# A two-layer mixer step: wider first sums, and the last 512 output columns with tokens on partitions

## The chip, the cores and the metric

The kernel runs on one core of one Trainium2 chip. The metric is the time of one execution in microseconds (us), the median of a few runs. A profile is one further execution, recorded by the hardware profiler. TensorE's clock has two levels in it, 1.2 GHz (a granted clock of 0.50) and 2.4 GHz (1.00).

## What is computed

The reference takes 128 context tokens and 256 noisy latent tokens through two layers each and returns both outputs and the new keys and values. One layer, cut to what matters here:

```python
shift, scale, gate = split(silu(cvec) @ w_mod[l] + b_mod[l], 3)     # 2048 x 6144
h = rmsnorm(x, norm_g[l]) * (1 + scale) + shift                     # x: tokens x 2048
chunks = split(h @ w_in[l], 11)                                     # 2048 x 5632
...                                                                 # Fourier, pooling, attention, convolution
y = concatenate([y_f, y_p, y_a, y_c]) @ w_out[l]                    # 2048 x 2048
x = x + gate * y
...
y_out = rmsnorm(x, final_g)                                         # after the second layer
```

`rmsnorm` divides every token by the root of the mean of its 2048 squares, so no output element can be finished before all 2048 columns of `x` are known for its token.

## The kernel before

All 384 tokens are worked on together, channels on the 128 partitions and tokens along the free dimension: `xT[g][:, b, :]` holds channels `(4 g + b) * 128` and on, for 384 tokens. Tokens 0 to 127 are the context, 128 to 383 the latent ones; `SEG` keeps their modulation apart. Weights come as tiles of 512 KB (`wtile`, L227): a DMA into one of 5 `raw` buffers, then `halves` (L211) makes a rounded high part on ScalarE (L116) and the remainder on VectorE (L107), each 128x512, in 6 buffers `hi` and 6 `lo`. A product is three matmuls: high by high, high by low, low by high (`mm3`, L439). Loads of weights and their splits are issued with a higher priority than their place in the program (`ahead`, L208).

**The start.** The constants and the four input groups `xT` are loaded, 3 matmuls of zeros (`idle<-still,ones`, L167) run while they come, and squares of the input are added in pairs on VectorE (`xsq`). `token_sums` (L421) then sums squares over partitions: the squares are the stationary operand, the moving one is a single column of ones, for each of 3 blocks of 128 tokens. There are eight such calls, two for each input group; a full float32 matmul leaves two records in the trace, so they are 48 records (`ssq`, L423). Of the first four modulation items (`mod_item`, L255; 16 matmuls, 32 records, and one 512 KB load each) two stand between the sums of groups 2 and 3, and two behind the last sums, beside the square root, the reciprocal and the diagonal on the other engines. A matmul with that diagonal (`bc`, L418) spreads the result over partitions, `make_h` (L427) builds the first `h`, and the first matmul `mm` follows. The queues of TensorE and of the DMA engine SP keep the written order up to the end of the first four chunks; VectorE and ScalarE keep it up to the first `h`. Behind that, a scheduler orders each engine by priority at compile time.

**The end.** In the second layer the output projection runs over 4 groups of 512 columns. Groups 0 to 2 go over 8 weight tiles each with 4 accumulators (one for 128 columns). Group 3 goes over its 4 blocks of 128 columns one by one, so that one block's work behind the matmuls runs beside the next block's matmuls. `finish_block` (L914) adds gate times result to `xT`, squares it, adds the squares up in `sacc`, multiplies by `final_g`, and transposes the block on TensorE to tokens on partitions (`otp`, L931). After the last block, the sums over partitions (`st`, L423) give the root for each token, twelve tiles of 128x512 are multiplied by its reciprocal (L980, L982), and twelve stores of 256 KB follow on SP's queue (L987).

Of the kernel before, what the change touches and what calls it, by code (L numbers as in the profile page):

```python
# [8 lines left out]
F32 = mybir.dt.float32  # L9
F32R = mybir.dt.float32r  # L10
AF = mybir.ActivationFunctionType
# [3 lines left out]
P = 128  # L15
# [40 lines left out]
def mixer_step(  # L56
    ctx: ExitStack,
    tc: tile.TileContext,
    x_in, cache_k, cache_v, consts, lam, packs,
    y_prompt, y_sample, new_k, new_v,  # L60
):
    nc = tc.nc
# [30 lines left out]
    def nm(s):  # L93
        uid[0] += 1
        return f"{s}_{uid[0]}"
# [16 lines left out]
    def act(out, a, func, **kw):  # L112
        nc.scalar.activation(out=out, in_=a, func=func, **kw)  # L113
# [19 lines left out]
    ones = one.tile([P, P], F32, tag="ones", name="ones")  # L133
    nc.vector.memset(ones, 1.0)
    still = gtile("H", "still", (P, 512))
    nc.vector.memset(still, 0.0)
    eps_t = one.tile([P, 1], F32, tag="eps", name="eps_t")
    nc.vector.memset(eps_t, EPS)
    cmod = one.tile([P, KC, 32], F32, tag="cmod", name="cmod")
# [16 lines left out]
    act(cmod[:, :, 0], cview("c_ctx"), AF.Silu)  # L156
    act(cmod[:, :, 1], cview("c"), AF.Silu)
    warm = one.tile([P, 1], F32, tag="warm", name="warm")
    act(warm, cmod[:, 0, 2:3], AF.Sqrt, bias=eps_t[:, 0:1])
    ncol = cview("norm_g")  # L160
    bcol = cview("b_mod")

# [7 lines left out]
    for g in range(4):  # L170
        sq = gtile("M", "xsq0")
        xsq.append(sq)
        act(sq[:, 0:2, :], xT[g][:, 0:2, :], AF.Square)
        tt(sq[:, 2:4, :], xT[g][:, 2:4, :], xT[g][:, 2:4, :], ALU.mult)
        tt(sq[:, 0:2, :], sq[:, 0:2, :], sq[:, 2:4, :], ALU.add)

# [78 lines left out]
    def mod_item(l, segs, k0, nk):  # L255
        nb = sum(n for _, _, n in segs)
        w = nb * P
        if prio[0]:
            raw = rawp.tile([P, nk, nb, P], F32, tag="raw", name=nm("mraw"))
        else:  # L260
            raw = gtile("Y", "mraw", (P, nk, nb, P))
        with ahead():
            def rows(a):
                parts = []
                for kind, b0, n in segs:
                    c0 = MOD.index(kind) * D + b0 * P
                    parts.append(a[l, k0 * P:(k0 + nk) * P, c0:c0 + n * P].reshape(nk, P, n, P))
                import numpy as np
                return np.concatenate(parts, axis=2).transpose(1, 0, 2, 3)

            nc.sync.dma_start(out=raw, in_=packs["w_mod"].take(rows, (P, nk, nb, P)))
        key = (l, segs)
        if k0 == 0:
            mod_ps[key] = mdp.tile([P, 512], F32, tag="md", name=nm("mod"))
        ps = mod_ps[key]
        for j in range(nk):
            for q in range(4):
                qs = slice(32 * q, 32 * q + 32)
                nc.tensor.matmul(ps[qs, 0:nb * 32].rearrange("p (b n) -> p b n", n=32), lhsT=cmod[:, k0 + j, :],  # L279
                                 rhs=raw[:, j, :, qs], start=(k0 + j == 0), stop=(k0 + j == KC - 1))  # L280
        if k0 + nk == KC:
            del mod_ps[key]
            T = one.tile([P, 8, 32], F32, tag="S", name=nm("T"))
            nc.vector.transpose(out=T[:, 0:nb, :].rearrange("p b n -> p (b n)"), in_=ps[:, 0:nb * 32])
            o = 0
            for kind, b0, n in segs:
                mod_store(l, kind, b0, n, T[:, o:o + n, 0:2])
                o += n
# [127 lines left out]
    def bcast_tokens(dg):  # L416
        bc = sm("bc")
        nc.tensor.matmul(bc[:, :NT], lhsT=ones, rhs=dg.rearrange("p t k -> p (t k)"))  # L418
        return bc

    def token_sums(st, acc, start=True, stop=True):  # L421
        for t in range(TB):
            nc.tensor.matmul(st[:, t:t + 1], lhsT=acc[:, t * P:(t + 1) * P], rhs=ones[:, 0:1], start=start and t == 0,  # L423
                             stop=stop and t == TB - 1)
        return st[:, 0:TB]

    def make_h(l, xT, bc, kcs, hh, hl):  # L427
        for kc in kcs:
# [355 lines left out]
    for l in range(DEPTH):  # L784
        if l == 0:
            groups = [(0, 1), (1, 1)] + [(k, 2) for k in range(2, KC, 2)]
            first = mod_group(0, *groups[0])
            ssq = sm("ssq")
            for g in range(4):
                if g == 3:  # L790
                    for it in first[:2]:
                        mod_item(*it)
                for i in range(2):
                    stat = token_sums(ssq, xsq[g][:, i, :], g == 0 and i == 0, g == 3 and i == 1)
            dg = diagonal(rstd_cols(stat, TB, 1.0 / D))
            for it in first[2:]:
                mod_item(*it)
        else:
            dg = diagonal(rstd_cols(stat, TB, 1.0 / D))
        bc_ps = bcast_tokens(dg)  # L800
        bc = one.tile([P, NT], F32, tag="bs", name=nm("bcs"))
        if l:
            copy_a(bc, bc_ps[:, :NT])
# [110 lines left out]
        def finish_block(g, b, ps, outs):  # L914
            kc = 4 * g + b
            x = xT[g][:, b, :]
            for a, z, vv in SEG:
                stt(x[:, a:z], ps[:, a:z], GT[l][:, kc, vv:vv + 1], x[:, a:z], ALU.mult, ALU.add)
            if kc == 0:
                act(sacc, x, AF.Square)  # L920
            else:
                sq = tmpp.tile([P, NT], F32, tag="t1", name=nm("xsq"))
                act(sq, x, AF.Square)
                if kc < KC - 1:
                    tt(sacc, sacc, sq, ALU.add)
                else:
                    tots.append(token_sums(tots[0], sq, start=False))
            if final:
                copy_a(x, x, scale=col("final_g", kc))
                for t in range(TB):  # L930
                    nc.tensor.transpose(outs[t][:, b * P:(b + 1) * P], x[:, t * P:(t + 1) * P], ident)  # L931

        otk = []
        for g in range(4):
            ps4 = [mmp.tile([P, 512], F32, tag="mm", name=nm("mm")) for _ in range(4)]
            if g < 3:
                for i, kt in enumerate(order):
                    hi, lo = wtile(w_src("w_out", l, 2 * kt, g * BR))
                    main_tile(ps4, hi, lo, (2 * kt, 2 * kt + 1), yh, yl, i == 0, i == 7)
                    pump()  # L940
            outs = [sm("otp") for _ in range(TB)] if final else None
            for b in range(4):
                if g == 3:
                    c0 = g * BR + b * P
                    for k0 in range(0, KC, 8):
                        hi, lo = wtile(w_src("w_out", l, k0, c0, 8, P), shape=(P, 8, P))
                        for j in range(8):
                            kc = k0 + j
                            mm3(ps4[b][:, :NT], hi(j), lo(j), yh[kc // 4][:, kc % 4, :],
                                yl[kc // 4][:, kc % 4, :], kc == 0, kc == KC - 1)  # L950
                        pump()
                        if b == 3 and k0 == 0:
                            tots.append(mdp.tile([P, 512], F32, tag="md", name=nm("st")) if final else sm("st"))
                            token_sums(tots[0], sacc, stop=False)
                finish_block(g, b, ps4[b], outs)
            if not final:
                nc.sync.dma_start(out=xd[g], in_=xT[g])
            elif g < 3:
                ot = gtile("H", "ot", (P, TB, BR))
                for t in range(TB):  # L960
                    nc.scalar.copy(out=ot[:, t, :], in_=outs[t])
                otk.append([ot[:, t, :] for t in range(TB)])
            else:
                otk.append(outs)
        pump(flush=True)
        rate["pe"] = rate["dve"] = 0.0
        if not final:
            share(1, [("gate", b0) for b0 in range(0, KC, 4)], NG)
            pe_mods(NB1)
        stat = tots[1]  # L970
        if not final:
            pe_mods(NB2)

    r = rstd_cols(stat, TB, 1.0 / D)
    n = 0
    for g in range(4):
        res = gtile("H", "res", (P, TB, BR))
        for t in range(TB):
            if n % 5 in (1, 3):
                copy_a(res[:, t, :], otk[g][t], scale=r[:, t:t + 1])  # L980
            else:
                nc.vector.tensor_scalar(out=res[:, t, :], in0=otk[g][t], scalar1=r[:, t:t + 1], scalar2=None,  # L982
                                        op0=ALU.mult)
            n += 1
            cs = slice(g * BR, (g + 1) * BR)
            dst = y_prompt[0, :, cs] if t == 0 else y_sample[0, (t - 1) * P:t * P, cs]
            nc.sync.dma_start(out=dst, in_=res[:, t, :])  # L987


def shape_constants():  # L990
# [115 lines left out]
```

## Time and profile before

| what | value |
|---|---|
| time, median of 3 runs | 1249.11 us (1248.88 to 1251.1) |
| time of the profiled execution | 1249.6 us |
| its span, first to last instruction | 1247.8 us |
| mean granted TensorE clock | 0.986 |
| TensorE busy in matmuls | 1223.0 us |
| VectorE, ScalarE busy | 922.4 us, 550.3 us |
| last matmul of the projection begins | 1233.37 us |

The profiled execution's own time is 1.8 us above its span. Moments below are counted from the span's start. A record's duration contains the filling of the array; what a matmul costs in a row of matmuls is read from the starts of consecutive ones.

### The profile page before, as it was taken

How to read it: one execution, taken by the hardware profiler on the slowest of the kernel's cores; microseconds unless marked ns; L12 is line 12 of the kernel's file. 1: busy time of each engine (PE TensorE's matmuls, PEld its weight loads, DVE VectorE, ACT ScalarE, POOL GpSimd, SP SyncE). 2: the span in 40 equal slices, each digit the busy share in tenths (PEclk: the TensorE clock that was granted, in tenths of full speed). 3: DMA queues.
4: the chain of work that ended last, by engine and by line, in shares of the span. 5: the costliest groups of instructions: out<-in, count | busy, mean ns of one | idle time of the engine just before them, and what ended most of it. 6: DMA issues, size and time to landing. Idle time of an engine off the chain costs nothing.

```text
span 1247.8 us, 22061 instructions
## 1 busy us (share of the span) xinstructions
PE 1223.0 (98%) x8558; PEld 1148.6 (92%) x8558; DVE 922.4 (74%) x1774; ACT 550.3 (44%) x1103; POOL 2.1 (0%) x34
## 2 busy tenths in 40 slices
PE   8999999999999999999999999999999999999995
PEld 6899998898999999999998999989999999999995
DVE  4787879999957956989968469997464895647452
ACT  3433333444547644433335433334455755344442
POOL 0000000000000000000000000000000000000000
PEclk6999999999999999999999999999999999999998
DMA  8988886553346766988945444444232563645322
GB/s 302 351 314 318 304 306 236 171 175 122 132 169 218 281 228 221 330 302 319 326 155 185 161 152 161 152 163 156 80 101 102 194 228 118 211 152 186 119 68 101
DMA packets 70712, 251.85 MB, mean 202 GB/s; under 512 B 7760, under 2 KB 8912, under 8 KB 70608
## 3 DMA queue, kind: packets, MB, share of 16 engines
q1 hardware_dynamic: 70608, 250.45, 57.1%
q8 instruction: 67, 1.10, 0.4%
q14 instruction: 37, 0.30, 0.1%
HBM read 243.08 MB, written 7.34 MB: 201 GB/s over the span
## 4 chain that ended last, share of the span: by engine, by line
PE 91%; DVE 5%; DMA 1%; ACT 1%; issue 1%; SPq 0%; DVEq 0%; ACTq 0%
PE mm L440 24%; PE mm L442 23%; PE mm L441 23%; PE mod L279 5%; PE mm L471 2%; PE mm L472 2%; PE mm L473 2%; DVE lo L107 1%; PE sp L440 1%; PE sp L441 1%; PE sp L442 1%; DVE cacc L110 1%; PE fb L712 1%; PE ssq L423 1%; PE aso L669 1%
## 5 line engine op out<-in xcount | busy, mean ns | idle before, releaser
L116 ACT ACTIVATE hi<-raw 128x512 fp32r<-128x512 f32 x498 | 308.9, 631 | 532.6 <-PE mm L441 345.8
L107 DVE TENSOR_TENSOR lo<-raw,hi 128x512 fp32r<-128x512 f32 x498 | 336.8, 688 | 212.7 <-ACT hi L116 203.6
L440 PE MATMUL mm<-hh,hi 128*128 128x384 f32 x1280 | 441.0, 345 | 3.7 <-ACT hh L113 3.7
L442 PE MATMUL mm<-hh,lo 128*128 128x384 f32 x1280 | 433.0, 338 | 2.5 <-DVE lo L107 2.5
L441 PE MATMUL mm<-hl,hi 128*128 128x384 f32 x1280 | 433.0, 338 | 0.0
L440 PEld LDWEIGHTS mm<-hh,hi 128*128 128x128 f32 x1280 | 242.0, 189 | 23.6 <-issue 10.1
L442 PEld LDWEIGHTS mm<-hh,lo 128*128 128x128 f32 x1280 | 242.3, 189 | 3.5 <-DVE lo L107 3.4
L441 PEld LDWEIGHTS mm<-hl,hi 128*128 128x128 f32 x1280 | 242.4, 189 | 1.0 <-DVE hl L110 0.4
L440 PE MATMUL mm<-yh,hi 128*128 128x384 f32 x512 | 173.6, 341 | 0.6 <-DVE xr L110 0.6
L441 PE MATMUL mm<-yl,hi 128*128 128x384 f32 x512 | 172.6, 337 | 0.0
L442 PE MATMUL mm<-yh,lo 128*128 128x384 f32 x512 | 172.5, 338 | 0.0
L110 DVE SCALAR_TENSOR_TENSOR macc<-sraw,cmod,macc 128x512 f32<-128x512 f32 x210 | 147.6, 746 | 6.3 <-DMA sraw<-in_w_mod_dram 6.3
L110 DVE SCALAR_TENSOR_TENSOR cacc<-u,cst,cacc 128x399 f32<-128x399 f32 x232 | 146.5, 631 | 6.0 <-ACT cacc L113 1.5
L440 PEld LDWEIGHTS mm<-yh,hi 128*128 128x128 f32 x512 | 96.4, 188 | 4.1 <-issue 2.5
L441 PEld LDWEIGHTS mm<-yl,hi 128*128 128x128 f32 x512 | 96.5, 188 | 0.0
L442 PEld LDWEIGHTS mm<-yh,lo 128*128 128x128 f32 x512 | 96.4, 188 | 0.0
L107 DVE TENSOR_TENSOR acc<-acc,mm 128x384 f32<-128x384 f32 x128 | 66.5, 553 | 26.9 <-PE mm L442 26.6
L279 PE MATMUL mod<-mraw,cmod 128*32 128x128 f32 (+2 forms) x1920 | 74.7, 296 | 0.0
L279 PEld LDWEIGHTS mod<-mraw,cmod 128*32 128x32 f32 x1920 | 49.7, 114 | 18.5 <-issue 10.6
L113 ACT ACTIVATE hh<-ht,AB 128x128 fp32r<-128x128 f32 x64 | 27.2, 451 | 27.5 <-DVE ht L110 26.8
L471 PE MATMUL mm<-hi,hh 128*128 128x512 f32 x96 | 38.3, 399 | 0.0
L472 PE MATMUL mm<-lo,hh 128*128 128x512 f32 x96 | 38.0, 396 | 0.0
(211 smaller groups left out, 944.0 us busy)
## 6 DMA issues: line engine op xcount, KB each, us to landing
raw<-in_w_in_dram SPq DMA_DIRECT2D x172, 512.0 KB, 4.2
mraw<-in_w_mod_dram SPq DMA_DIRECT2D x136, 512.0 KB, 4.6
raw<-in_w_out_dram SPq DMA_DIRECT2D x64, 512.0 KB, 4.2
sraw<-in_w_mod_dram SPq DMA_DIRECT2D x56, 512.0 KB, 5.6
xT<-in_x_dram SPq DMA_DIRECT2D x4, 768.0 KB, 6.8
xr<-in_x_dram SPq DMA_DIRECT2D x4, 768.0 KB, 6.5
xd<-xr SPq DMA_DIRECT2D x4, 768.0 KB, 5.1
xr<-xd SPq DMA_DIRECT2D x4, 768.0 KB, 5.8
```

The costliest lines, as they stand in the source:

```text
L107: (eng or nc.vector).tensor_tensor(out=out, in0=a, in1=b, op=op)
L110: nc.vector.scalar_tensor_tensor(out=out, in0=a, scalar=s, in1=b, op0=op0, op1=op1)
L113: nc.scalar.activation(out=out, in_=a, func=func, **kw)
L116: nc.scalar.activation(out=out, in_=a, func=AF.Copy, scale=scale)
L279: nc.tensor.matmul(ps[qs, 0:nb * 32].rearrange("p (b n) -> p b n", n=32), lhsT=cmod[:, k0 + j, :], rhs=raw[:, j, :, qs], start=(k0 + j == ...
L423: nc.tensor.matmul(st[:, t:t + 1], lhsT=acc[:, t * P:(t + 1) * P], rhs=ones[:, 0:1], start=start and t == 0, stop=stop and t == TB - 1)
L440: nc.tensor.matmul(ps, lhsT=wh, rhs=ah, start=start, stop=False)
L441: nc.tensor.matmul(ps, lhsT=wh, rhs=al, start=False, stop=False)
L442: nc.tensor.matmul(ps, lhsT=wl, rhs=ah, start=False, stop=stop)
L471: nc.tensor.matmul(ps3[t], lhsT=hh[g][:, kb, ts], rhs=hi(j), start=st, stop=False)
L472: nc.tensor.matmul(ps3[t], lhsT=hh[g][:, kb, ts], rhs=lo(j), start=False, stop=False)
L473: nc.tensor.matmul(ps3[t], lhsT=hl[g][:, kb, ts], rhs=hi(j), start=False, stop=sp)
```

## The change

There are two parts, and small moves with the first. At the start, the sums' moving operand becomes 128 columns of ones, of whose equal results one is read; all sums stand together, three modulation items follow them, and the fourth stands behind the matmul with the diagonal. The zeros for the idle matmuls are written by GpSimd, and the instruction that makes ScalarE load the table of the square root stands behind the first square. At the end, group 3 is computed with tokens on partitions: `y` is the stationary operand and 512 columns of weights the moving one, for token blocks 0 and 1 in a first pass over the 8 weight tiles and block 2 in a second. The second pass starts with the three tiles still held in the split buffers and loads the other five again. Gate, `final_g` and the old `x` of these columns are brought to that layout by 20 transposes and one small load. Each token block is finished, scaled and stored for all four groups once its pass is over.

```diff
-    nc.vector.memset(still, 0.0)
+    nc.gpsimd.memset(still, 0.0)
...
-    act(warm, cmod[:, 0, 2:3], AF.Sqrt, bias=eps_t[:, 0:1])
...
         act(sq[:, 0:2, :], xT[g][:, 0:2, :], AF.Square)
+        if g == 0:
+            act(warm, cmod[:, 0, 2:3], AF.Sqrt, bias=eps_t[:, 0:1])
...
-    def token_sums(st, acc, start=True, stop=True):
+    def token_sums(st, acc, start=True, stop=True, n=1):
         for t in range(TB):
...
+            nc.tensor.matmul(st[:, t * n:(t + 1) * n], lhsT=acc[:, t * P:(t + 1) * P], rhs=ones[:, 0:n],
+                             start=start and t == 0, stop=stop and t == TB - 1)
...
             for g in range(4):
-                if g == 3:
-                    for it in first[:2]:
-                        mod_item(*it)
                 for i in range(2):
-                    stat = token_sums(ssq, xsq[g][:, i, :], g == 0 and i == 0, g == 3 and i == 1)
+                    stat = token_sums(ssq, xsq[g][:, i, :], g == 0 and i == 0, g == 3 and i == 1, P)
             dg = diagonal(rstd_cols(stat, TB, 1.0 / D))
-            for it in first[2:]:
+            for it in first[:3]:
                 mod_item(*it)
...
         bc_ps = bcast_tokens(dg)
+        if l == 0:
+            mod_item(*first[3])
...
         for g in range(4):
+            if final and g == 3:
+                break
...
+    l, G = DEPTH - 1, 3
+    gb = gtile("H", "gb", (P, 3, BR))
+    nc.sync.dma_start(out=gb[:, 2, :], in_=final_b)
+    for v in range(2):
+        gw = gtile("H", "gw", (P, 4, P))
+        nc.vector.tensor_copy(out=gw, in_=GT[l][:, 4 * G:4 * G + 4, v].unsqueeze(2).to_broadcast([P, 4, P]))
+        ps = sm("gbp")
+        for b in range(4):
+            nc.tensor.transpose(ps[:, b * P:(b + 1) * P], gw[:, b, :], ident)
+        nc.scalar.copy(out=gb[:, v, :], in_=ps)
+    xt = gtile("H", "xt", (P, TB, BR))
+    for t in range(TB):
+        ps = sm("xtp")
+        for b in range(4):
+            nc.tensor.transpose(ps[:, b * P:(b + 1) * P], xT[G][:, b, t * P:(t + 1) * P], ident)
+        nc.scalar.copy(out=xt[:, t, :], in_=ps)
+    rest = tiny.tile([P, TB], F32, tag="rest", name="rest")
+    part = token_sums(mdp.tile([P, 512], F32, tag="md", name="st"), sacc)
+    nc.vector.tensor_scalar(out=rest, in0=part, scalar1=1.0 / D, scalar2=EPS, op0=ALU.mult, op1=ALU.add)
...
+    def tokens_tile(w, kt, ts, first, last):
+        hi, lo = w
+        for j in range(2):
+            kc = 2 * kt + j
+            for t in ts:
+                ah = yh[kc // 4][:, kc % 4, t * P:(t + 1) * P]
+                al = yl[kc // 4][:, kc % 4, t * P:(t + 1) * P]
+                nc.tensor.matmul(ps3[t], lhsT=ah, rhs=hi(j), start=first and j == 0, stop=False)
+                nc.tensor.matmul(ps3[t], lhsT=ah, rhs=lo(j), start=False, stop=False)
+                nc.tensor.matmul(ps3[t], lhsT=al, rhs=hi(j), start=False, stop=last and j == 1)
+
+    def finish_tokens(t):
+        z = xt[:, t, :]
+        tt(zt[:, t, :], ps3[t], gb[:, min(t, 1), :], ALU.mult)
+        tt(z, zt[:, t, :], z, ALU.add)
+        act(zt[:, t, :], z, AF.Square, accum_out=own[:, t:t + 1])
+        s = tiny.tile([P, 1], F32, tag="sqt", name=nm("sq"))
+        act(s, own[:, t:t + 1], AF.Sqrt, scale=1.0 / D, bias=rest[:, t:t + 1])
+        r = tiny.tile([P, 1], F32, tag="rst", name=nm("rs"))
+        nc.vector.reciprocal(out=r, in_=s)
+        for g in range(4):
+            if g == 1:
+                copy_a(ots[g][:, t, :], ots[g][:, t, :], scale=r)
+            elif g < 3:
+                nc.vector.tensor_scalar(out=ots[g][:, t, :], in0=ots[g][:, t, :], scalar1=r, scalar2=None,
+                                        op0=ALU.mult)
             else:
+                stt(z, z, r, gb[:, 2, :], ALU.mult, ALU.mult)
...
+    ps3 = [mmp.tile([P, 512], F32, tag="mm", name=nm("mm")) for _ in range(TB)]
+    ws = []
+    for i, kt in enumerate(order):
+        ws.append(wtile(srcs[i]))
+        tokens_tile(ws[i], kt, (0, 1), i == 0, i == 7)
+    for t in (0, 1):
+        finish_tokens(t)
+    again = (5, 6, 7, 0, 1, 2, 3, 4)
+    for n, i in enumerate(again):
+        w = ws[i] if n < 3 else wtile(srcs[i])
+        tokens_tile(w, order[i], (2,), n == 0, n == 7)
+    finish_tokens(2)
```

## Rows read from the trace of the kernel before

**Rows 1.** The page: busy time of each engine, and TensorE's clock in 40 slices.
```profile
PE 1223.0 (98%) x8558; PEld 1148.6 (92%) x8558; DVE 922.4 (74%) x1774; ACT 550.3 (44%) x1103; POOL 2.1 (0%) x34
...
PEclk6999999999999999999999999999999999999998
```

**Rows 2.** Chain of waits, start of the span (start us, us, what).
```profile
8.00 7.27 PE ssq L423 x36
...
19.78 1.86 PE mod L279 x64
21.65 1.59 PE bc L418 x2
...
24.60 0.69 PE mm L440
...
29.21 1.03 PE mod L279 x64
```

**Rows 3.** Windows of 2 us: busy time by engine, clock, DMA share, GB/s.
```profile
8.00:10.00 2.00, 2.00 (x12) 2.00 (x13) 1.90 (x3) 0.96 (x2) 0.00 (x0) 0.66 1.01 421
...
26.00:28.00 2.00, 2.00 (x8) 2.00 (x7) 0.00 (x0) 1.16 (x3) 0.00 (x0) 0.50 0.31 127
28.00:30.00 2.00, 2.00 (x65) 1.56 (x67) 0.69 (x1) 1.24 (x3) 0.00 (x0) 0.72 0.00 0
...
44.00:46.00 2.00, 2.00 (x36) 1.75 (x38) 1.92 (x4) 0.00 (x0) 0.00 (x0) 1.00 1.03 410
```

**Rows 4.** Timeline of the start: zero matmuls, a table load, the last input squares.
```profile
1.59 4.64 PE L167 MATMUL idle<-still,ones 128*128 128x512 f32 x6 [1.59 <-DVE still L136]
...
4.63 1.28 ACT L113 ACT_TABLE_LOAD   x1
...
12.79 0.96 DVE L107 TENSOR_TENSOR xsq<-xsq 128x768 f32<-128x768 f32 x1
```

**Rows 5.** Chain of waits around 314 us: float32 matmuls of 128 columns.
```profile
313.82 1.34 PE aso L669 x12
```

**Rows 6.** Chain of waits, last matmuls to the reciprocal root.
```profile
1226.46 0.34 PE otp L931 x3
...
1229.56 0.17 PE mm L441
...
1233.37 0.19 PE mm L442
...
1236.10 0.19 DVE rs L407
```

**Rows 7.** Chain of waits in `v_chunk`: first and 28th matmul of 512 columns.
```profile
201.32 0.23 PE mm L471
...
207.62 0.23 PE mm L471
```

**Rows 8.** Groups of instructions (busy us, mean ns), whole span.
```profile
L107 DVE TENSOR_TENSOR lo<-raw,hi 128x512 fp32r<-128x512 f32 x498 | 336.8, 688 | 212.7 <-ACT hi L116 203.6 <-PE mm L442 7.8
...
L110 DVE SCALAR_TENSOR_TENSOR macc<-sraw,cmod,macc 128x512 f32<-128x512 f32 x210 | 147.6, 746 | 6.3 <-DMA sraw<-in_w_mod_dram 6.3
...
L107 DVE TENSOR_TENSOR u<-u,fa 128x512 f32<-128x512 f32 x8 | 5.5, 684 | 2.0 <-PE fa L692 1.9
...
L982 DVE TENSOR_SCALAR res<-ot,rs 128x512 f32<-128x512 f32 x5 | 2.1, 480 | 0.0
...
L116 ACT ACTIVATE res<-ot,rs 128x512 f32<-128x512 f32 x4 | 2.6, 710 | 0.2 <-DVE rs L407 0.2
```

**Rows 9.** Windows of 1 us while the outputs are stored (columns of rows 3).
```profile
1237.00:1238.00 1.00, 0.00 (x0) 0.00 (x0) 1.00 (x4) 1.00 (x3) 0.00 (x0) 0.73 0.31 119
...
1246.00:1247.00 1.00, 0.00 (x0) 0.00 (x0) 0.00 (x0) 0.00 (x0) 0.00 (x0) 0.50 0.04 12
```

**Rows 10.** The stores' time from issue to landing, and the page's weight loads.
```profile
DMA to landing us min/median/max: 2.3/3.3/5.8
...
raw<-in_w_out_dram SPq DMA_DIRECT2D x64, 512.0 KB, 4.2
```

More of the change, by code (lines that the diff above doesn't have):

```diff
@@ L58, in mixer_step @@
     tc: tile.TileContext,
-    x_in, cache_k, cache_v, consts, lam, packs,
+    x_in, cache_k, cache_v, consts, lam, final_b, packs,
     y_prompt, y_sample, new_k, new_v,
@@ L419, in bcast_tokens @@
         return bc
-    def token_sums(st, acc, start=True, stop=True):
+    def token_sums(st, acc, start=True, stop=True, n=1):
         for t in range(TB):
-            nc.tensor.matmul(st[:, t:t + 1], lhsT=acc[:, t * P:(t + 1) * P], rhs=ones[:, 0:1], start=start and t == 0,
-                             stop=stop and t == TB - 1)
-        return st[:, 0:TB]
+            nc.tensor.matmul(st[:, t * n:(t + 1) * n], lhsT=acc[:, t * P:(t + 1) * P], rhs=ones[:, 0:n],
+                             start=start and t == 0, stop=stop and t == TB - 1)
+        return st[:, 0:TB] if n == 1 else st[:, 0:TB * n].rearrange("p (t n) -> p t n", n=n)[:, :, 0]
     def make_h(l, xT, bc, kcs, hh, hl):
@@ L923, in finish_block @@
                 act(sq, x, AF.Square)
-                if kc < KC - 1:
+                if final or kc < KC - 1:
                     tt(sacc, sacc, sq, ALU.add)
@@ L931, in finish_block @@
                     nc.tensor.transpose(outs[t][:, b * P:(b + 1) * P], x[:, t * P:(t + 1) * P], ident)
-        otk = []
+        ots = []
         for g in range(4):
+            if final and g == 3:
+                break
             ps4 = [mmp.tile([P, 512], F32, tag="mm", name=nm("mm")) for _ in range(4)]
@@ L952, in mixer_step @@
                         if b == 3 and k0 == 0:
-                            tots.append(mdp.tile([P, 512], F32, tag="md", name=nm("st")) if final else sm("st"))
+                            tots.append(sm("st"))
                             token_sums(tots[0], sacc, stop=False)
@@ L957, in mixer_step @@
                 nc.sync.dma_start(out=xd[g], in_=xT[g])
-            elif g < 3:
+            else:
                 ot = gtile("H", "ot", (P, TB, BR))
@@ L961, in mixer_step @@
                     nc.scalar.copy(out=ot[:, t, :], in_=outs[t])
-                otk.append([ot[:, t, :] for t in range(TB)])
-            else:
-                otk.append(outs)
+                ots.append(ot)
         pump(flush=True)
@@ L969, in mixer_step @@
             pe_mods(NB1)
-        stat = tots[1]
         if not final:
+            stat = tots[1]
             pe_mods(NB2)
[L974 to L980, printed above, removed]
-            else:
-                nc.vector.tensor_scalar(out=res[:, t, :], in0=otk[g][t], scalar1=r[:, t:t + 1], scalar2=None,
-                                        op0=ALU.mult)
-            n += 1
+    l, G = DEPTH - 1, 3
@@ new lines, in mixer_step @@
+    rest = tiny.tile([P, TB], F32, tag="rest", name="rest")
+    part = token_sums(mdp.tile([P, 512], F32, tag="md", name="st"), sacc)
+    nc.vector.tensor_scalar(out=rest, in0=part, scalar1=1.0 / D, scalar2=EPS, op0=ALU.mult, op1=ALU.add)
+    own = tiny.tile([P, TB], F32, tag="own", name="own")
+    zt = gtile("H", "zt", (P, TB, BR))
+    def tokens_tile(w, kt, ts, first, last):
[8 more added lines that the diff above has]
+                nc.tensor.matmul(ps3[t], lhsT=al, rhs=hi(j), start=False, stop=last and j == 1)
@@ L985, in mixer_step @@
             cs = slice(g * BR, (g + 1) * BR)
             dst = y_prompt[0, :, cs] if t == 0 else y_sample[0, (t - 1) * P:t * P, cs]
-            nc.sync.dma_start(out=dst, in_=res[:, t, :])
+            nc.sync.dma_start(out=dst, in_=ots[g][:, t, :] if g < 3 else z)
+    srcs = [w_src("w_out", l, 2 * kt, G * BR) for kt in order]
+    ps3 = [mmp.tile([P, 512], F32, tag="mm", name=nm("mm")) for _ in range(TB)]
[3 more added lines that the diff above has]
+        tokens_tile(ws[i], kt, (0, 1), i == 0, i == 7)
@@ L1085 @@
         "in_lambda_dram": _np.broadcast_to(i["diff_lambda"].reshape(1, -1), (P, i["diff_lambda"].size)),
+        "in_final_dram": _np.broadcast_to(i["final_g"][3 * BR:], (P, BR)),
     }
```

## The prediction

> **What bounds the kernel now.** I read the page first. TensorE is busy for 98% of the span, so its queue sets the time wherever work is dense, and its clock is low in the first and the last slice alone [rows 1]. The change touches these two ends, so the rest was left aside and each end was read from its chain of waits.
>
> At the start the chain is nearly all TensorE's: the sums from 8.00 us, modulation, the matmul with the diagonal, the first `mm` at 24.60 [rows 2]. The windows show the granted clock falling in 8 to 10 us (mean 0.66), at 0.50 in 26 to 28, and back at 1.00 in 28 to 30 (mean 0.72, so at about 29.1) [rows 3]. Zero matmuls had run from 1.59 to 6.23 [rows 4]; then came a pause and one-column sums, and the clock fell. It came back 4.5 us after the first matmuls of 384 columns. The reader is to see that 20 us of TensorE's chain run at the lower level. The same windows show a second limit: the DMA engines stand idle around 26 to 30 (shares 0.31 and 0.00), waiting for modulation buffers that TensorE has not yet read, and are full later (1.03 in 44 to 46) [rows 3].
>
> At the end, the last matmul starts at 1233.37 and the reciprocal ends at 1236.28 [rows 6]. Then come the stores: hardly any traffic before 1237.7, none after 1246 [rows 9], and the span ends at 1247.8. That is 14.4 us behind the last matmul, 8.3 of them for twelve stores, 0.69 each.
>
> **The start, step by step.** A float32 matmul of 128 columns costs 1.34/12 = 0.112 us a record at full clock [rows 5], so 0.224 at half; the one-column records cost 7.27/36 = 0.202 at half [rows 2]. Wider operands thus hardly lengthen the sums, because the weight load already sets that pace. What they do to the clock is not in the trace. If dense sums act as the dense matmuls did, the clock is up 4.5 us after 8.00, at 12.5. Twenty records are done by then; 28 at 0.112 end at 15.6. The last inputs, ready at 13.75 [rows 4], allow 15.1 at best. Three modulation items at 0.52 (1.03 for two at full clock [rows 2]) give 17.2. The diagonal must be ready too, which takes at most the 1.86 us of the two items that cover it now [rows 2]: I take 17.4. The diagonal's matmul at half its 1.59 gives 18.2, the fourth item 18.7. From a modulation item's end to the first `mm` it is now 24.60 - 21.65 = 2.95 us [rows 2], an upper bound, since that time also holds the diagonal's matmul. The first `mm` comes at 21.6, 3.0 us earlier. The twelve matmuls up to 29.21 take 4.6 us now and 12 x 0.173 = 2.1 at full clock, which would make it 5.5.
>
> That cannot all be kept. After 30 us the loads are the limit, and TensorE's earlier arrival helps them only by filling their idle time: 1.4 us of 26 to 28 and 2.0 of 28 to 30 [rows 3]. I take **-3.4 us**; it holds even if the clock drops again before the first `mm`, since 3.0 is left then. The bounds are -5.5 and, if the sums never raise the clock, 48 x 0.224 to 18.8, then 2.8, 1.6, 0.9 and 2.95 to 27.0: +2.4.
>
> The small moves cost nothing. The sums wait for squared inputs at 8.00, while the zero matmuls end at 6.23 [rows 2, 4], so GpSimd may be 1.7 us slower with the zeros. The table load now falls between the first and second group's squares; the second group's sums stand behind the first's on TensorE, which covers it. SP's loads keep their order. Without that cover the load would cost its 1.28 us [rows 4].
>
> **The end, step by step.** *Matmuls.* Now 192 of 384 columns at (1233.37 - 1229.56)/22 = 0.173 us [rows 6]: 33.25. Then 96 + 48 of 512 columns at (207.62 - 201.32)/27 = 0.233 [rows 7]: 33.6. That is **+0.35**: the second pass repeats no products, only loads.
>
> *Transposes.* Nine leave TensorE's queue ahead of the last matmul, 20 come, at 0.34/3 = 0.113 [rows 6]: +1.2, and 0.1 for switching: **+1.3** (lower bound 1.2; upper bound below, as a rival). The six `st` records ahead of the end are exchanged for six, at no difference; the six behind the last matmul vanish into the tail below. The Trainium skill (TensorE: Matmul & The Clock Gate, Part 4) speaks against transposes on TensorE: about 275 ns each in a kernel's context. By that, an estimate, 20 would cost 5.5 us. The row here disagrees, at 0.113 from start to start.
>
> *VectorE in the second pass.* The pass lasts 48 x 0.233 = 11.2 us. Three tiles are split already; five are split during it, ten VectorE instructions of 0.69 [rows 8], 6.9 us. Finishing blocks 0 and 1 adds, for each, two products and sums at 0.68 and 0.69, a reciprocal of 0.18, two scalings at 0.48 and one of 0.75 [rows 6, 8]: 3.26, or 6.5 together. So 13.4 us of work stand against 11.2 us and the 0.5 that block 0 is ready early. Block 2's own chain queues behind what is left: **+1.5**, bounds 0 (the rest fits into gaps of block 2's chain) and 4 (splits held up behind the finishing, so that TensorE waits too).
>
> *The tail.* From the last matmul: 0.2 to hand over, 0.68 + 0.69 on VectorE, 0.71 for the square (the nearest 128x512 row of ScalarE), root and reciprocal 0.45 [rows 6, 8], some 0.25 between them: 3.0, as now. Then 0.48 + 0.48 + 0.75 on VectorE, with ScalarE's 0.71 beside them, and the last store is issued at 4.7. It lands 2.3 to 3.3 us later [rows 10]; four stores at 0.69 from 4.4 on fit in that. With the 1.8 us that now follow the last store, 8.8 to 9.8, so 9.3 against 14.4: **-5.1**. The cover for the other eight stores, 5.5 us, is the second pass.
>
> **Sum.** -3.4 + 0.35 + 1.3 + 1.5 - 5.1 = -5.35 us. The profiled execution took 1249.6 (1.8 above its span), so 1244.25; the median of the runs shown is 0.5 lower: **1243.8 us**. A difference within 0.2% (2.5 us, so 1246.6 to 1251.6) is about what a measurement of this kernel can't tell from none.
>
> **Rivals.**
>
> *The second pass becomes VectorE's.* If its order puts finishing ahead of splits, TensorE stalls 4 us and the rest of blocks 0 and 1 still delays block 2 by 1.7: 5.7 for the 1.5, 1248.0. For it: 13.4 us of work in 11.7. Against: weight splits have the higher priority, and three tiles of cover.
>
> *The sums do not raise the clock.* +2.4 for the -3.4: 1249.6. For it: nothing ran long enough at 128 columns in this stage to show it. Against: at 0.224 a record the array gets columns almost without pause, as with the matmuls after which the clock came back [rows 2, 3].
>
> *The start gives back what it gains.* If the loads of the next group are as late as now for another reason (queue order, VectorE's order of sums and splits), 1 us is left: 1246.2. For it: DMA is full at 44 to 46 [rows 3].
>
> *Slower: stores ahead of weights on SP.* SP issues in one order. If the eight stores of blocks 0 and 1 stand ahead of the five reloaded tiles, those are issued some 8 us into the second pass, land 4.2 later [rows 10], and are split by 13.5, where the first is needed after 4.2: a stall of about 9 us, 1252.8. It is slower from a stall of 7.9 on. Against: the loads have priority, five raw buffers let them run ahead, and tile 7's split, which frees the last buffer, is done in the first pass.
>
> *The transposes come at their price alone.* They come in five groups of four, each group into its own buffer, which ScalarE must copy out. If TensorE stands at each group for one such copy, at 0.71 (ScalarE's 128x512 row [rows 8]), that is 3.5 us more, 1247.3. The figure of the Trainium skill above, as an estimate, would come to 3.2 more. Against: the transposes between matmuls now take 0.34 for three [rows 6].
>
> **How the numbers follow.** My forecast's case has 0.54, with its own range of 1240.2 (start -5.5, no stall) to 1246.1 (start -2.5, stall 3). VectorE's bound has 0.10, the clock 0.11, the start given back 0.14, SP's order 0.06, the transposes 0.05. The range goes from 1240.2 to 1249.6: outside are SP's order, half of the clock's case and about 0.05 at the edges of mine, 0.17 in all. Faster: 0.54, 0.13 of the start given back, 0.03 of the transposes: 0.70. Slower: SP's 0.06, 0.03 of the clock, 0.02 of VectorE's bound: 0.11. The rest, 0.19, is within 0.2%.
>
> **What would show it.** Right: granted clock near 1.00 from about 12 to 13 us on; last `ssq` record at 15 to 16.5; first `mm` at 20 to 22.5; no empty DMA window before 40 us; in the second pass few waits of TensorE on `lo`; eight stores issued before the last matmul; 8.8 to 9.8 us from that matmul's start to the span's end. Wrong: `ssq` records still at 0.2 us after 14 us (the clock's case); TensorE waiting on `lo` or on `raw` for several us near the end (VectorE's or SP's); waits ahead of the new transposes; the last matmul later than 1233.4 minus the start's gain plus 3 us.

## The result and the profile after

The changed kernel takes 1242.47 us (median of 4 runs, 1241.56 to 1243.97), beside 1248.99 for the kernel before (4 runs, 1248.71 to 1251.1). The ratio is 0.9945, with a 95% interval of 0.9928 to 0.9963: 6.5 us faster, where 5.35 were forecast. The profiled execution took 1241.56 us, its span is 1239.7, which is 8.1 less than before.

The page of the changed kernel: busy time, and TensorE's clock in 40 slices (before: [rows 1]). TensorE still fills 98% of the span. The clock's first slice rose from 6 to 8, the last stayed at 8.

```profile
PE 1216.6 (98%) x8512; PEld 1136.2 (92%) x8512; DVE 929.2 (75%) x1785; ACT 555.7 (45%) x1116; POOL 2.5 (0%) x35
...
PEclk8999999999999999999999999999999999999998
```

The chain of waits at its start (start us, us, what), to be laid beside [rows 2]:

```profile
13.67 1.60 PE ssq L424 x12
15.27 1.48 PE mod L280 x96
16.75 0.84 PE bc L419 x2
17.59 0.63 PE mod L280 x32
...
21.53 0.69 PE mm L442
...
24.46 0.32 PE mm L441
...
25.18 1.03 PE mod L280 x64
```

Its windows of 2 us (columns of [rows 3]):

```profile
8.00:10.00 2.00, 2.00 (x11) 2.00 (x11) 1.79 (x3) 1.25 (x3) 0.00 (x0) 0.50 1.01 424
10.00:12.00 2.00, 2.00 (x15) 2.00 (x15) 1.90 (x3) 0.95 (x2) 0.00 (x0) 0.72 1.00 410
...
18.00:20.00 2.00, 0.18 (x14) 0.01 (x2) 1.69 (x7) 0.66 (x2) 0.00 (x0) 1.00 1.04 398
20.00:22.00 2.00, 0.91 (x2) 0.65 (x3) 1.48 (x4) 1.14 (x3) 0.00 (x0) 0.84 1.03 409
22.00:24.00 2.00, 2.00 (x8) 2.00 (x8) 0.00 (x0) 0.94 (x3) 0.00 (x0) 0.50 1.03 394
24.00:26.00 2.00, 2.00 (x69) 1.76 (x67) 0.69 (x1) 1.46 (x4) 0.00 (x0) 0.81 0.65 255
26.00:28.00 2.00, 2.00 (x27) 1.91 (x16) 0.00 (x0) 0.96 (x2) 0.00 (x0) 1.00 0.63 182
```

The clock stood at 0.50 in 8 to 10 and came back at about 11.1 (a mean of 0.72 over 10 to 12), while the wide sums ran. The sums end at 15.27, after which the modulation items take 0.49 each. In 18 to 20 TensorE is all but idle: it waits for the chain on VectorE and ScalarE that makes the first operand. There the clock falls a second time, at about 21.4 (0.84 over 20 to 22), and eight of the first twelve matmuls take 0.32 each, until 24.8, where 0.17 is full pace. No window is empty of DMA traffic any more. The next modulation item starts at 25.18, where it started at 29.21 [rows 2]: 4.0 us earlier.

At the end the last matmul starts at 1230.28, and the end of the span is 9.42 us later. Before, it was 14.6 us: by the timeline the last matmul started at 1233.20 there. The 1233.37 of the chain [rows 6] is 0.17 later, since a chain shows each piece only from the end of the one before it. The two last matmuls in the timeline, before and after:

```profile
1233.20 0.34 PE L442 MATMUL mm<-yh,lo 128*128 128x384 f32 x1
```

```profile
1230.28 0.39 PE L1006 MATMUL mm<-hi,yl 128*128 128x512 f32 x1
```

The chain of waits around and behind the second of them:

```profile
1230.27 0.66 DVE xt L110
1230.93 0.61 DVE zt L107
...
1232.29 0.73 ACT zt L113 x2
...
1233.37 0.17 DVE rs L1016
...
1233.57 0.48 DVE ot L1021
...
1234.45 0.66 DVE xt L110
```

Block 2's product follows a scaling of block 1 without a gap, at 1230.9 in the chain (1230.85 in the timeline); product, sum, square, root and reciprocal take until 1233.5, and the scalings until 1235.1.

SP's queue in the timeline (start us, us, what), twelve stores:

```profile
1226.44 2.54 SPq L1027 DMA_DIRECT2D out_dram<-ot  x3
1229.31 0.33 SPq L1027 DMA_DIRECT2D out_dram<-xt  x1
1229.90 1.33 SPq L1027 DMA_DIRECT2D out_dram<-ot  x3
1231.33 0.43 SPq L1027 DMA_DIRECT2D out_dram<-xt  x1
1234.08 1.30 SPq L1027 DMA_DIRECT2D out_dram<-ot  x3
1235.48 0.41 SPq L1027 DMA_DIRECT2D out_dram<-xt  x1
```

Eight stores are issued by 1231.8, around the last matmul, and only the four of block 2 stand behind that block's reciprocal, which ends at 1233.5. Before, all twelve stood behind the one reciprocal, which ended at 1236.3.

The difference in span, 8.1 us, is then 4.0 at the start, 5.2 in the tail, less 1.4 for TensorE's work on the last 512 columns. That lasted 36.3 us from its first matmul to the last one's start before (1196.92 to 1233.20 in the timeline), and 37.7 after (1192.60 to 1230.28). The 0.3 left over comes between 540 and 770 us: the lead of 4.0 falls to 2.9 there and rises to 4.3, as the kernel before lost its clock once more in its profile (a mean of 0.57 over 664 to 668) and the changed one did not (1.00).

### The profile page after: what moved, and what is told of

Read it like the earlier page. It is cut to its first block, busy times and chain, and to the rows that moved or that the text cites. A ratio compares the mean times of both kernels' runs of the same rounds, so it can differ in the third digit from the quotient of the medians.

```text
span 1239.7 us, 22018 instructions
## 1 busy us (share of the span) xinstructions
PE 1216.6 (98%) x8512; PEld 1136.2 (92%) x8512; DVE 929.2 (75%) x1785; ACT 555.7 (45%) x1116; POOL 2.5 (0%) x35
## 4 chain that ended last, share of the span: by engine, by line
PE 88%; DVE 7%; DMA 2%; issue 1%; ACT 1%; SPq 0%; DVEq 0%; ACTq 0%
PE mm L441 23%; PE mm L442 22%; PE mm L443 22%; PE mod L280 5%; DVE lo L107 2%; PE mm L472 2%; PE mm L473 2%; PE mm L474 2%; DMA sraw<-in_w_mod_dram 1%; PE sp L441 1%; PE sp L442 1%; PE sp L443 1%; DVE cacc L110 1%; PE fb L713 1%; PE aso L670 1%
## 5 line engine op out<-in xcount | busy, mean ns | idle before, releaser
L116 ACT ACTIVATE hi<-raw 128x512 fp32r<-128x512 f32 x508 | 314.7, 630 | 537.8 <-PE mm L442 338.9
L107 DVE TENSOR_TENSOR lo<-raw,hi 128x512 fp32r<-128x512 f32 x508 | 343.0, 687 | 207.6 <-ACT hi L116 197.9
L441 PE MATMUL mm<-yh,hi 128*128 128x384 f32 x448 | 151.7, 340 | 1.4 <-DVE xr L110 1.4
L443 PE MATMUL mm<-yh,lo 128*128 128x384 f32 x448 | 150.7, 337 | 0.0
L442 PE MATMUL mm<-yl,hi 128*128 128x384 f32 x448 | 150.6, 336 | 0.0
L441 PEld LDWEIGHTS mm<-yh,hi 128*128 128x128 f32 x448 | 84.2, 188 | 5.0 <-issue 3.4
L442 PEld LDWEIGHTS mm<-yl,hi 128*128 128x128 f32 x448 | 84.3, 188 | 0.0
L443 PEld LDWEIGHTS mm<-yh,lo 128*128 128x128 f32 x448 | 84.1, 188 | 0.0
L113 ACT ACTIVATE hh<-ht,AB 128x128 fp32r<-128x128 f32 x64 | 27.3, 451 | 25.4 <-DVE ht L110 24.8
```

The costliest lines, as they stand in the source:

```text
L116: nc.scalar.activation(out=out, in_=a, func=AF.Copy, scale=scale)
L441: nc.tensor.matmul(ps, lhsT=wh, rhs=ah, start=start, stop=False)
L442: nc.tensor.matmul(ps, lhsT=wh, rhs=al, start=False, stop=False)
L443: nc.tensor.matmul(ps, lhsT=wl, rhs=ah, start=False, stop=stop)
```

## Experiments

Ratios are to the kernel before on the same chip, with 95% intervals; its medians there were 1249.51 us for the first four kernels, 1250.65 for the next four, 1249.67 for the last two. Two times of the trace serve as marks: the start of the modulation item behind the first twelve matmuls (29.21 before, 25.18 after), and the issue of the store of `new_k`, far behind the start, at 198.5 before and 194.5 after.

**e1_start_alone: the first part by itself.** The kernel before with the hunks for the zeros, the table load, the wide sums and the order of the items.

> The start of the change alone, the old end kept. If the two parts add up, this gives the start's share as the traces show it, 3.8 us at the first mm and 4.0 at 29 us: about 1245 us, with the granted clock back at 1.00 around 11 us, first mm near 21 us, and 14.4 us from the start of the last matmul to the end of the span. If the start's gain only shows together with the new end (its earlier finish swallowed by waits later in the kernel), the time stays within 1 us of the kernel before, 1249.

Measured: 1244.63 us (1242.49 to 1248.54, 11 runs), ratio 0.9966 [0.9954, 0.9979], 4.9 us. In this profile the clock was 1.00 at the start throughout; the item starts at 23.68, and the store stands at 192.3, 6.2 earlier than before. The tail is as before, 14.6.

The line of that store in this run:

```profile
L585 SPq DMA_DIRECT2D out_dram<-acc x1: 632/632/632, 192.3 to 192.3; - x1
```

What the start gains at 24 us (5.5) is still there at 192. It is more than the -3.4 that the sum allowed it.

**e2_end_alone: the second part by itself.** The changed kernel with those hunks undone.

> The end of the change alone, the old start kept. Theory, all gain of the end is the shorter tail behind the last matmul, paid with some 1.2 us on TensorE: first mm at 24.6 us as before, 37.6 us from the first matmul of the last 512 columns to the start of the last one (36.4 before), then 9.4 us (14.4 before), together -3.8: about 1245.3 us. Rival, the end profits from the earlier start (loads that have time to run ahead): less than 2 us, 1247 or more.

Measured: 1245.58 us (1243.59 to 1248.37, 9 runs), 0.9965 [0.9953, 0.9977], 3.9 us. From the first matmul of the last 512 columns (1196.61) to the last one's start (1234.29) it is 37.7, and the tail is 9.41. The parts add: 4.9 + 3.9 = 8.8, and the whole gained 6.5 (4.6 to 9.0 by its interval), and 9.3 as e8. Neither part pays for the other.

**e3_one_column: the whole change, the sums one column wide.**

```
-                    stat = token_sums(ssq, xsq[g][:, i, :], g == 0 and i == 0, g == 3 and i == 1, P)
+                    stat = token_sums(ssq, xsq[g][:, i, :], g == 0 and i == 0, g == 3 and i == 1)
```

> The changed kernel with one column of ones in the first sums, all else of the change kept (order of the modulation items, zeros from GpSimd, later table load). Theory, the width brings the clock back: it stays at 0.50 from about 8.6 us until some 4 us after the first dense matmuls, the sums end at 17.4 (48 records at 0.202 from 7.7), the first mm comes at about 25, and the time is near 1247 us. Rival, the gain comes from the order and the earlier sums: first mm at 22 us or before, and about 1243 us.

Measured: 1246.01 us (1244.07 to 1249.21, 12 runs), 0.9975 [0.9963, 0.9987]: about that of the end alone. Its chain of waits at the start:

```profile
11.76 5.28 PE ssq L424 x24
17.05 2.71 PE mod L280 x96
19.76 1.49 PE bc L419 x2
...
28.57 1.03 PE mod L280 x64
```

The clock was at 1.00 until about 10.8 and then at 0.50 to 21. The last 24 records of the sums pass at 0.22 each, where the dense ones of the changed kernel take 0.112; the items take 0.90 against 0.49, the diagonal's matmul 1.49 against 0.84. The width of the sums is what keeps the clock up or brings it back, and moving the items without it wins nothing that the medians show.

**e4_hold_clock: the second fall taken away.** Three zero matmuls of 512 columns behind the fourth item, where TensorE is idle.

```
+            fz = sm("fill")
+            for _ in range(HOLD):
+                nc.tensor.matmul(fz, lhsT=ones, rhs=still, start=True, stop=True)
```

> The changed kernel with three more matmuls of zeros (128x512, into a tile that nobody reads) between the fourth modulation item and the first mm, where TensorE now idles 2.6 us and the clock falls once more. Theory, this second fall is what kept the start from its full 5.5 us: the clock stays at 1.00, the twelve matmuls behind the first mm take 2.1 to 2.4 us instead of 4.3, and the time falls by about 2 us to 1240.5. Rival, the limit that the prediction named, the loads' idle time: the matmuls are faster, but TensorE waits longer for weights before 60 us, and the time stays at 1242 to 1243. If the zeros hold up the first mm instead, it comes later than 21 us.

Measured: 1241.12 us (1239.71 to 1244.08, 6 runs), 0.9938 [0.9923, 0.9954]. The clock stays at 1.00 from 11.6 to 544 us; the item starts at 23.90, and the store stands at 192.5, 6.0 earlier than before and 2.0 earlier than in the first profile of the changed kernel. So the twelve matmuls' second half, which the sum gave up to the loads, arrives and is kept, as far as 192 us. The medians do not tell this kernel from the changed one: this profile lost time again further on (TensorE waits 2.12 us for VectorE up to 543.8, and the clock falls there and near 664), and its span is 1242.1.

**e5_one_pass: the end's second pass taken away.** All three token blocks run through one pass over the eight weight tiles.

```
+        tokens_tile(wtile(srcs[i]), kt, (0, 1, 2), i == 0, i == 7)
+    for t in range(TB):
         finish_tokens(t)
```

> The changed kernel with the last 512 columns in one pass over the weights: each of the 8 tiles is used for all three token blocks, and all three are finished behind it. TensorE does the same 144 matmuls, so the first pass costs nothing more. Theory, the second pass is worth what it hides, the finishing of two blocks (6.5 us on VectorE) and eight stores (5.5 us): the last matmul starts at about the same time, but the span ends some 15 us behind it instead of 9.4, and the time is about 5 us above the changed kernel, 1247. Rival, the layout itself shortens the tail (fewer steps, no transposes behind the last matmul): at most 2 us above it.

Measured: 1247.68 us (1245.41 to 1249.29, 11 runs), 0.998 [0.997, 0.999]. Its last matmul starts at 1230.63; its stores in the timeline:

```profile
1234.21 1.62 SPq L1027 DMA_DIRECT2D out_dram<-ot  x3
...
1240.95 0.59 SPq L1027 DMA_DIRECT2D out_dram<-xt  x1
```

TensorE needs 37.7 us for the columns, as in two passes, so loading five tiles again costs it nothing. The tail is 14.57 us, 5.15 more and as long as before the change (14.6): all that the end wins comes from the second pass, which hides eight stores. On the same chip this kernel takes 6.3 us more than e8. The new layout without the second pass shortens nothing at the end.

**e6_hold_and_warm: both falls taken away.** Besides e4's lines, five zero matmuls at the start instead of three.

> The changed kernel with five instead of three matmuls of zeros at the very start, so that TensorE has no pause before the first sums, and with the three zero matmuls ahead of the first mm. Theory, both falls of the clock come from TensorE's pauses at 6 to 8 and 18 to 21 us: the clock stays at 1.00 from its first rise on in every profile, the first mm is at 20.8 or somewhat before, and the median is 1240 to 1241, with no run above 1243 unless a later fall adds to it. Rival, the clock falls during the sums in any case (the dense work must go on longer): no better than with the three zeros alone, 1241.1. If the zeros hold up the sums, the last sums end later than 15.3.

Measured: 1241.19 us (1239.93 to 1242.69, 5 runs), 0.9928 [0.9913, 0.9944]. The clock is 1.00 from 4 to 1230 us, the item starts at 23.86. But TensorE waited 1.52 us for a modulation load up to 193.5 and 1.84 us for VectorE (`xr`) up to 545.5, and the span is 1240.9. It can't be told from the changed kernel.

**e7_width_alone: one argument.** The kernel before, its order of items and all else kept, with the wide sums alone.

> The kernel before with only the width changed: 128 columns of ones in the first sums, the old order of the modulation items, zeros from VectorE, old place of the table load, old end. Theory, the width alone carries the start's gain: the clock is back at 1.00 by 12 us, the sums end by 16.5, the first mm comes at 19.5 to 21, and the time is that of the start alone, 1244 to 1245. Rival, the order of the items has a share of its own: first mm later than 21.5, and 1246 or more.

Measured: 1244.83 us (1242.68 to 1245.47, 5 runs), 0.9956 [0.9942, 0.997], 5.8 us: as much as the whole start (4.9 in e1), within the intervals. Its chain and the timeline's first `mm`:

```profile
13.56 1.09 PE mod L279 x64
14.65 1.55 PE ssq L423 x12
```

```profile
19.86 0.45 PE L440 MATMUL mm<-hh,hi 128*128 128x384 f32 x1 [1.60 <-ACT hh L113]
```

The sums end 0.9 later than in the changed kernel, at 16.2, since two items stand ahead of the last group's. The first `mm` nevertheless comes 0.9 earlier, 19.86 against 20.81: with two items done, fewer stand between the sums and the first operand. The new order of items is thus a small loss, which the width covers; e9 tries it against e8.

**e8_changed_again: the changed kernel once more**, for its spread.

> The changed kernel once more, to stand beside the others on the same chip: 1241.5 to 1244 us, as measured first. Its profile tells whether the two falls of the clock, at about 8 and 21 us, come in every execution or in some: theory, their moments shift from run to run, and the time with them by 1 to 2 us.

Measured: 1241.34 us (1238.97 to 1242.84, 5 runs), 0.9931 [0.9915, 0.9947]. The windows of this execution, for the stretch in which the first one had lost its clock:

```profile
20.00:22.00 2.00, 0.94 (x4) 0.69 (x5) 1.45 (x4) 1.11 (x3) 0.00 (x0) 1.00 1.04 413
22.00:24.00 2.00, 2.00 (x37) 1.75 (x39) 0.27 (x1) 1.79 (x5) 0.00 (x0) 1.00 1.03 394
```

Here the clock did not fall at 8 nor at 21, the item starts at 23.69 (5.5 earlier than before), the store stands at 192.4 and the span is 1237.1, 2.6 less than in the first profile of the same kernel. The loads' share of 20 to 42, in one window each for the kernel before, the first profile of the changed one, and this one:

```profile
20.00:42.00 22.00, 20.59 (x319) 17.56 (x311) 9.65 (x26) 12.96 (x29) 0.00 (x0) 0.79 0.74 251
```

```profile
20.00:42.00 22.00, 20.01 (x292) 18.06 (x296) 11.06 (x25) 11.71 (x26) 0.00 (x0) 0.92 0.89 323
```

```profile
20.00:42.00 22.00, 20.04 (x330) 17.89 (x331) 11.26 (x26) 12.15 (x27) 0.00 (x0) 1.00 0.96 351
```

The idle time of the DMA engines is 22 x 0.26 = 5.7 us before, 22 x 0.11 = 2.4 in the first profile after, and 22 x 0.04 = 0.9 here. The clock of this stretch and the loads' share rise together; which of the two sets the other, these windows don't show.

**e9_old_order_warm: what e7 points to.** The changed kernel with the items in their old order, and five zero matmuls at the start.

> A candidate put together from the runs so far: the changed kernel with the old order of the modulation items (two before the last sums, two behind, none behind the matmul with the diagonal) and five zero matmuls at the start. Theory, the old order brings the first mm 0.9 us earlier (19.9 against 20.8, as the width alone did) since nothing then stands between the diagonal's matmul and h, and the clock is at 1.00 from 8 us to the first mm: 1240 to 1241 us, 0.5 to 1 below the changed kernel's 1241.3 to 1242.5. Rival, the spread between executions (falls of the clock, late loads further on) is larger than what is left at the start: not to be told from the changed kernel.

Measured: 1241.24 us (1238.29 to 1243.66, 6 runs), 0.9929 [0.9913, 0.9944]. The clock was 1.00 from 4 to 32 us, and the item starts at 22.85, 0.84 earlier than in e8 (and 1.0 earlier than in e6, which has the five zeros, the new order and the zeros of e4). That is the order's price again. It does not last: the store stands at 192.3, as in e8 (192.4). The modulation item that starts at 126.51 before, in the kernel before, e8 and e9:

```profile
126.51 1.96 PE L279 MATMUL mod<-mraw,cmod 128*32 128x128 f32 x64
```

```profile
121.08 1.95 PE L280 MATMUL mod<-mraw,cmod 128*32 128x128 f32 x64
```

```profile
120.12 1.95 PE L280 MATMUL mod<-mraw,cmod 128*32 128x128 f32 x64
```

Up to there e8 is 5.4 ahead of the kernel before and e9 6.4, as at the start. Then TensorE waits for the first operand of the next product in the kernel before and in e9:

```profile
133.27 0.42 PE L440 MATMUL mm<-hh,hi 128*128 128x384 f32 x1 [0.44 <-ACT hh L113]
```

```profile
127.06 0.41 PE L441 MATMUL mm<-hh,hi 128*128 128x384 f32 x1 [0.62 <-ACT hh L113]
```

In both, the chain of that wait goes back over VectorE and ScalarE to the load of a weight tile, 8.0 and 9.1 us long; e8 has no such wait. Behind it e8 is 6.1 ahead and e9 6.2. In the median no better version is shown.

**e10_no_zeros: the zero matmuls left out** (`WARM` from 3 to 0), so that nothing runs on TensorE before the sums.

> The changed kernel without the matmuls of zeros at the start. If the dense sums alone bring the clock back, as the theory has it, the records of the sums begin at the pace of half clock, 0.22 us, from 7.7 us, the clock reaches 1.00 between 10 and 13 us in the profile, the last sums end at 15.2 to 16, since the last group's inputs come at 13.6 anyway, and the time is that of the changed kernel within 1 us. Rival, the sums only keep up a clock that the zeros have raised: the clock stays at 0.50 up to the first mm, which comes near 25, and the time is 1246 or more.

Measured: 1242.26 us (1240.57 to 1246.42, 6 runs), 0.9943 [0.9927, 0.9959]. Windows of half a microsecond, of the sums alone (us, busy PE and records, clock, DMA share, GB/s):

```profile
8.00:8.50 0.50, 0.50 (x4) 1.00 0.97 406
...
10.50:11.00 0.50, 0.50 (x5) 1.00 1.02 418
11.00:11.50 0.50, 0.50 (x7) 1.00 0.98 401
```

and the first of them in e8, where the zeros had run:

```profile
8.00:8.50 0.50, 0.50 (x7) 1.00 1.00 418
```

The count takes in each record that touches the stretch: in the trace the records follow each other at 0.213 us up to 10.8 and at 0.112 from 11.0 on. So four in a stretch is half pace and seven is full, and the sums started at half pace and came to full pace at about 11, with nothing before them: dense sums raise the clock by themselves, and the zeros are not needed for that. The last sums still end at 15.29, held by their inputs.

## Why the prediction was right, and where it was off

**The clock at the start.** Right. The sums brought the clock back at 11.1, against 12.5 as forecast, and ended at 15.27 against 15.6. The rival "the sums do not raise the clock" is refuted by the first profile after, by e4 and above all by e10, where the clock rises while the wide sums run. In e1, e7 and e8 it was up when they began and stayed up, and in e3 it fell under the narrow ones. What ended the sums at 15.27 was not their pace but the last inputs, ready at 13.6: close to the forecast's best case of 15.1. The forecast took 0.202 us for a narrow record at half clock; that mean holds six records at full clock, and start to start it is 0.112 at full and 0.213 at half, for one column and for 128 alike. The first `mm` came at 20.81, forecast 21.6, 3.8 us earlier than before.

**"That cannot all be kept."** This is the step that failed, and in its mechanism. The sum first found 5.5 us and then cut them to 3.4, since behind 30 us the loads were to be the limit and their idle time the most that could be won. In the first profile the gain is 4.0, which looks as if a limit were there; but its windows show another cause, the clock's second fall across the twelve matmuls. That 4.0 came near 3.4 is luck. Without that fall (e1, e4, e8) the item starts 5.3 to 5.5 earlier, as the sum had found, and the store at 192 us is 6.0 to 6.2 earlier. Had the loads been the limit, TensorE would wait longer for split weights the earlier it arrives. It does not; its first such wait, before and in e8:

```profile
43.32 0.45 PE L442 MATMUL mm<-hh,lo 128*128 128x384 f32 x1 [0.90 <-DVE lo L107]
```

```profile
37.81 0.45 PE L443 MATMUL mm<-hh,lo 128*128 128x384 f32 x1 [0.90 <-DVE lo L107]
```

The two that follow take 1.16 and 0.40 in both. So e8's lead of 5.5 and e9's of 6.4 are whole at 120 us (see e9). Nor is the idle time a bound when it is counted over a longer stretch: over 20 to 42 it was 5.7 us, and e9's lead is larger. Waits behind a load are few and short on the way to 192 us. The largest is the one near 130 us: it takes 0.2 from e9's lead, and as e8 lacks it and the kernel before has it, e8's lead rises from 5.4 to 6.1. Why it comes in some executions was not tried. The prediction's other guess, that 3.0 is left if the clock falls again, was low by 1.0. By medians the start is worth 4.9 (e1) to 5.8 us (e7). The rival "the start gives back what it gains" is refuted by the same store.

**Small moves at no cost.** Half right. Order of loads and zeros show no cost in the chain. The table load does stand in it, with 1.28 us at 6.44 between two squares of the input, and VectorE waits 0.21 for the second of them; but the last inputs are ready at 13.6, no later than before (13.75). The new order of the items, which the sum took as part of the gain, costs 0.8 to 0.9 at the first `mm` (e7 against the changed kernel, e9 against e8).

**Matmuls and transposes.** Forecast +0.35 and +1.3, measured +1.4 together. The chain has them one by one:

```profile
1201.41 0.44 PE gbp L983 x4
...
1202.08 0.44 PE gbp L983 x4
1202.52 1.33 PE xtp L989 x12
```

That is 0.11 for each of the twenty, 2.2 together, with no wait for ScalarE's copies between them: the rival "at their price alone" is refuted. The record of one transpose lasts longer than that step (ns, minimum, median and maximum):

```profile
L983 PE MATMUL gbp<-cst,gw x8: 272/273/273, 1201.2 to 1202.2; 128*128 128x128 f32 x8
```

The Trainium skill (TensorE: Matmul & The Clock Gate, Part 4) gives about 275 ns for a 128x128 transpose in one kernel's context, as a duration. The trace agrees with it as a duration, at 273 ns. The prediction laid that duration beside a step from start to start and called them at odds; what twenty in a row cost the queue is the step, 0.11.

**VectorE in the second pass.** The mechanism was there, its size was not: +1.5 forecast, some 0.35 measured. VectorE is busy for 4.90 of 5 us from 1220 and 4.93 of 5 from 1225, as its 13.4 us of work in the pass had said. But block 2's product starts at 1230.85 behind a last scaling of block 1, where 0.2 to hand over had put it at 1230.5. TensorE never waits for a split in that pass; it steps at 0.233 us to the end. Neither VectorE's rival nor SP's came about: SP's last load of a weight tile is issued at 1212.50, ahead of the first store at 1226.44.

**The tail.** Right in its mechanism: 9.42 us, VectorE's 0.35 among them, against 9.3 without it. That it is so close is in part luck: the last store goes out 5.2 us behind the last matmul (forecast 4.7) and lands 3.1 later (2.3 to 3.3), but from there to the end it is 1.1 us, where 1.8 was taken over from before; there, too, it was 1.0, from the last landing at 1246.8. "Eight stores issued before the last matmul" was too strict, for only five are; the other three go out by 1231.8, and their traffic is through (a DMA share of 0.11 in 1234 to 1235) before the last ones need the queue. e5 shows that the second pass is all of this gain.

**The sum.** By medians of the parts, the start gave 4.9 where 3.4 was forecast and the end 3.9 where 1.95 was (0.35 + 1.3 + 1.5 - 5.1). The errors of the parts have one sign: the start was cut by a limit that was not there, and the end was charged too much: for TensorE 1.65 where it was 1.4, and for VectorE and the tail together 10.8 us behind the last matmul where it was 9.42. The median of 1242.47 lies 1.3 below the forecast, and that of e8 2.5 below.

## What to carry to other kernels

Where a matmul of one column takes as long as one of 128, as in these sums (0.112 us a record at full clock, 0.213 at half, for both), try the wider moving operand: here it cost nothing and kept the clock up, or brought it up, for what follows. Before a resource is called the limit of a gain, look at the waits for it: if they do not grow when the waiting engine arrives earlier, it is not the limit there, however full it looks. A tail of scalings and stores is best shortened by finishing one part of the output while TensorE still works on the rest, and loading five weight tiles a second time cost TensorE nothing here (37.7 us with and without).

## What the runs showed of the hardware

The clock's falls come at different moments in executions of one program: at 8 and 21 us in the first profile after, at neither in e8. The whole span differs by 2.6 us between these two, of which some 2.1 stand at 192 us. In all twelve profiles TensorE waits 1.9 to 2.2 us for `hh` near 660 us, and in four of them (before, e1, e2, e4) the clock falls there. The Trainium skill (TensorE: Matmul & The Clock Gate, Part 1) says that the point of a transition varies from run to run, because the chip's window doesn't begin with the kernel. The traces agree that it varies; why is shown by no run here.

The granted clock's column can read 1.00 when the pace is half. In e10 it does so from 8 to 10.8 us, while records follow each other at 0.213 us, and the same column shows 0.50 for that pace in the first profile after. It seems to show 1.00 until the first change is recorded; the pace of records tells more there. The Trainium skill (TensorE: Matmul & The Clock Gate, Part 1) warns against trusting such records by themselves, and this trace agrees for the stretch ahead of the first change.

Waits of TensorE further on differ between executions: near 545 us it waits for `xr` on VectorE 0.30 us in e1, 1.84 in e6 and 2.24 in e7, and up to 193.5 e6 alone waits 1.52 for a load. With them, a gain of under 2 us at the start, which the traces show plainly, can't be seen in a median of five or six runs.
